# Seven products instead of eight in the down-projection of a hybrid decoder layer

## The chip, the cores and the metric

The kernel runs on one core of a Trainium2 chip. The metric is the device time of one execution in microseconds, as a median of several runs. A core has five engines that run side by side, each with a queue that it works through in order: TensorE (PE, matrix products, with its weight loads listed as PEld), VectorE (DVE), ScalarE (ACT), GpSimd (POOL) and SyncE (SP), which here starts nearly all DMA transfers. SBUF is the on-chip memory, 128 partitions wide; PSUM holds eight banks of 128 x 512 32-bit sums, into which TensorE alone accumulates matrix products.

## What is computed

One decoder layer with sequence length 2048, width 1024 and feed-forward width 2816, all in float32:

```python
def swiglu(h, w_gate_up, w_down):
    gu = h @ w_gate_up
    g, u = jnp.split(gu, 2, axis=-1)
    return (jax.nn.silu(g) * u) @ w_down
...
        h = modulate(rmsnorm(x, norm1_w[layer]), shift1, scale1)
        x = x + gate1[:, None, :] * hybrid_mixer(
            h, positions, w_in[layer], conv_w[layer], conv_b[layer], dt_bias[layer],
            a_log[layer], d_skip[layer], attn_sinks[layer], ssm_norm_w[layer], w_out[layer])
        h = modulate(rmsnorm(x, norm2_w[layer]), shift2, scale2)
        x = x + gate2[:, None, :] * swiglu(h, w_gate_up[layer], w_down[layer])
    return rmsnorm(x, final_norm_w)
```

The mixer (window attention beside a state-space scan, then an output projection by `w_out`) is left as it is by the change. What changes is the last product, `(silu(g) * u) @ w_down`, of 2048 x 2816 by 2816 x 1024, and the order of work around it.

## The kernel before

Everything is held transposed: features on the 128 partitions, tokens along the free axis. The 2048 tokens are four blocks of T = 512, and two blocks make a pair. Width 1024 is 8 slices of 128, the feed-forward width 22 slices (NF) of 128.

**Products.** A float32 operand is split into a high part (rounded to the matrix format, by ScalarE) and a low part (what is left, by VectorE or GpSimd). A product of a 128 x 128 weight with a 128 x 512 operand is three matmuls: high x high, high x low, low x high (`mm3`, lines 274 to 277). So each weight chunk of 128 x 512 from HBM costs a load of 256 KB into one of five `raw` buffers, one ScalarE and one VectorE or GpSimd operation into one of six `w` buffers, and then serves twelve matmuls.

**Gate and up.** `quads` runs 22 `quad`s for each pair of blocks. A quad makes slice f of the activations of both blocks, and does the 2 x 2 product of halves (two halves of the width 1024, two blocks) by seven products instead of eight, with sums of weights (`s1` to `s4`) and of tokens (`t1` to `t4`) in the manner of Strassen and Winograd. Its four sums stand in PSUM banks `pa` to `pd`. In the first pair these are always the same four `d` banks (the mixer's attention and scan of the last blocks run beside it and use the other four); in the second pair quads alternate between two sets of four. `u2`, `u3`, `c22`, `g1`, `g2`, `c12` are temporaries out of a ring of eight (`tmp`). The results are `g1` (first block, line 1010) and `g2` (second block, line 1005), and are written to DRAM (`act_d`, lines 1006 and 1011).

**Down.** `down(b)` runs for one block after the other: 6 groups of 4 (at last 2) activation slices, and in each group 8 columns of output. `acts` loads a group's activations and splits them (lines 1037 to 1040, ring `a` of 8); `columns` multiplies them with the split weights of that group and column, and at the end of every group adds the sum, times the gate, to the residual `x2` in SBUF (line 1075 on VectorE, reading PSUM). Block 0 writes its split weights to DRAM (`down_d`), block 1 reads them back, blocks 2 and 3 split anew. At the last group the squares of `x2` are summed for the final norm (`square_into`, ScalarE and GpSimd); `final` makes the root, spreads it over the partitions by a product with ones, scales, and writes the output. In block 3 the last group is done in two halves of 256 tokens, with VectorE in exactly the written order.

**Order.** `main` generators are stepped, and beside each step `beside` advances the generators in `sides` by a given ratio. A planner then orders each engine's instructions by when its own model of time has them ready, with the program's order as priority; inside `manual_schedule` the named engines keep the written order. From the first gate/up pair on, the order is: gate/up of blocks 0 and 1 with the attention and scan of the last blocks beside it, then the output projection of block 2 (`first_output`); `down` of blocks 0 and 1, with the rest of that projection, the projection of block 3 (`second_output`) and the second pair's operands (`first_operands`, `last_operands`) beside it; gate/up of blocks 2 and 3; `down` of blocks 2 and 3. `out_proj` (line 807) uses weights that block 0 split and kept in DRAM (512 KB per chunk, line 262).

## Time and profile before

| | us |
|---|---|
| median of three runs | 2342.59 (2342.11 to 2344.79) |
| span of the profiled execution | 2337.7 |
| gate/up of blocks 0 and 1, with mixer work beside it | 749.3 to 1322.6 |
| down of blocks 0 and 1, with output projections and operands beside it | 1322.6 to 1648 |
| gate/up of blocks 2 and 3 | 1648 to 2065.9 |
| down of blocks 2 and 3 | 2065.9 to 2323.8 |
| what is left after the last product | 2323.8 to 2337.7 |

The span runs from the first to the last instruction of one profiled execution. The page shows no other time for that execution than its span; the runs' times are taken apart from it, and the median is 4.9 above the span. The stages overlap a little at their edges, and the limits in the table are the starts of the first products of each. In rows of the profile, `d<-a,w` is a product of activations and down-projection weights, `d<-b,w` one of gate/up operands, and a name of the form L1075 is line 1075 of the kernel; `t<-act` is a load of an activation slice into a temporary.

### The profile page before, as it was taken

The numbers are of one execution on the slowest core, as the hardware profiler recorded it, in microseconds if no ns is written. First come the engines' busy times: TensorE is split into PE (matmuls) and PEld (weight loads), VectorE is DVE, ScalarE is ACT, GpSimd is POOL, SyncE is SP. The second block draws the span as 40 slices with busy tenths as digits, with TensorE's granted clock in tenths as the row PEclk, the third lists the DMA queues.
The fourth block names the chain that finished last, engine by engine and source line by source line (L and its number), as shares of the span: only waits on it lengthen the run. The fifth ranks groups of instructions, "written<-read, shape, count | busy, mean of one in ns | idle before, by whom it ended". The sixth has DMA issues, their size and how long they took to land. (4 is left out here: it accounts for less than half of the span.)

```text
span 2337.7 us, 33382 instructions
## 1 busy us (share of the span) xinstructions
PE 2233.3 (96%) x11252; PEld 1849.7 (79%) x11252; DVE 1444.3 (62%) x2607; ACT 943.0 (40%) x1976; POOL 1189.9 (51%) x1191
## 2 busy tenths in 40 slices
PE   6878989999999999999999999999999999999998
PEld 5778778888879788887877788877788888888777
DVE  8987975773568856676664353387644454454544
ACT  4564543654346645333333232223333333333332
POOL 2556433553223855687784332326666666653442
PEclk9998999999999999999999999999999999999999
DMA  8899987777888422323334998797422222263452
GB/s 295 291 327 306 304 260 250 252 247 252 293 268 314 135 86 73 108 86 95 95 100 154 337 359 307 238 340 244 140 82 81 82 82 81 81 226 104 134 182 64
DMA packets 271531, 453.14 MB, mean 194 GB/s; under 512 B 24960, under 2 KB 71040, under 8 KB 271360
## 3 DMA queue, kind: packets, MB, share of 16 engines
q1 hardware_dynamic: 270784, 450.48, 58.0%
q8 instruction: 89, 1.46, 0.3%
q14 instruction: 82, 0.67, 0.1%
q10 hardware_dynamic: 576, 0.52, 0.1%
HBM read 329.21 MB, written 121.70 MB: 193 GB/s over the span
## 5 line engine op out<-in xcount | busy, mean ns | idle before, releaser
L951 PE MATMUL d<-b,w 128*128 128x512 f32 x924 | 367.6, 399 | 1.3 <-POOL w L850 1.3
L950 PE MATMUL d<-b,w 128*128 128x512 f32 x924 | 366.8, 397 | 0.3 <-POOL b L880 0.3
L949 PE MATMUL d<-b,w 128*128 128x512 f32 x924 | 364.8, 398 | 1.1 <-DVE t L977 0.6
L849 ACT ACTIVATE w<-raw 128x512 fp32r<-128x512 f32 x264 | 166.0, 631 | 389.3 <-PE d L277 181.3
L275 PE MATMUL d<-a,w 128*128 128x512 f32 (+1 forms) x720 | 281.3, 393 | 6.1 <-ACT a L1039 3.2
L277 PE MATMUL d<-a,w 128*128 128x512 f32 (+1 forms) x720 | 282.8, 393 | 0.0
L276 PE MATMUL d<-a,w 128*128 128x512 f32 (+1 forms) x720 | 280.9, 390 | 1.1 <-POOL a L844 0.6
L1075 DVE SCALAR_TENSOR_TENSOR x<-d,mod,x 128x512 f32<-128x512 f32 (+1 forms) x182 | 130.8, 724 | 169.3 <-PE d L277 167.4
L850 DVE TENSOR_TENSOR w<-raw,w 128x512 fp32r<-128x512 f32 x198 | 184.8, 934 | 60.9 <-ACT w L849 57.0
L951 PEld LDWEIGHTS d<-b,w 128*128 128x128 f32 x924 | 174.1, 188 | 41.9 <-POOL w L850 1.7
L949 PEld LDWEIGHTS d<-b,w 128*128 128x128 f32 x924 | 174.4, 189 | 41.3 <-ACT t L980 1.2
L950 PEld LDWEIGHTS d<-b,w 128*128 128x128 f32 x924 | 174.5, 189 | 39.5 <-POOL b L880 0.7
L850 POOL TENSOR_TENSOR w<-s,w 128x512 fp32r<-128x512 f32 x132 | 187.3, 1420 | 31.5 <-ACT w L849 31.1
L849 ACT ACTIVATE w<-s 128x512 fp32r<-128x512 f32 x176 | 111.0, 632 | 221.1 <-PE d L951 163.1
L850 POOL TENSOR_TENSOR w<-raw,w 128x512 fp32r<-128x512 f32 x66 | 88.1, 1335 | 194.8 <-ACT w L849 173.5
L275 PE MATMUL d<-w,hl 128*128 128x256 f32 (+1 forms) x592 | 176.4, 298 | 7.3 <-ACT hl L326 5.6
L277 PE MATMUL d<-w,hl 128*128 128x256 f32 (+1 forms) x592 | 171.5, 290 | 2.7 <-DVE hl L327 2.7
L276 PE MATMUL d<-w,hl 128*128 128x256 f32 (+1 forms) x592 | 171.5, 290 | 0.0
L285 POOL TENSOR_TENSOR acc<-acc,t 128x512 f32<-128x512 f32 x70 | 95.8, 1369 | 147.7 <-ACT t L284 147.2
L275 PEld LDWEIGHTS d<-a,w 128*128 128x128 f32 x720 | 135.7, 189 | 40.0 <-ACT a L1039 5.4
L276 PEld LDWEIGHTS d<-a,w 128*128 128x128 f32 x720 | 136.3, 189 | 33.5 <-DVE a L844 1.1
L277 PEld LDWEIGHTS d<-a,w 128*128 128x128 f32 x720 | 135.8, 189 | 30.7 <-issue 0.7
(399 smaller groups left out, 5394.0 us busy)
## 6 DMA issues: line engine op xcount, KB each, us to landing
raw<-in_wgu_dram SPq DMA_DIRECT2D x176, 256.0 KB, 2.7
raw<-in_wd_dram SPq DMA_DIRECT2D x132, 256.0 KB, 2.9
w<-w_x SPq DMA_DIRECT2D x48, 512.0 KB, 5.1
w<-w_o SPq DMA_DIRECT2D x48, 512.0 KB, 5.2
act<-t SPq DMA_DIRECT2D x88, 256.0 KB, 2.1
wd<-w SPq DMA_DIRECT2D x88, 256.0 KB, 4.4
t<-act SPq DMA_DIRECT2D x88, 256.0 KB, 4.8
w<-wd SPq DMA_DIRECT2D x88, 256.0 KB, 4.2
```

The source lines that it names most:

```text
L275: nc.tensor.matmul(out, ahi, bhi, start=first, stop=False)
L276: nc.tensor.matmul(out, ahi, blo, start=False, stop=False)
L277: mm3.last = nc.tensor.matmul(out, alo, bhi, start=False, stop=last)
L285: eng.tensor_tensor(acc, acc, sq, ALU.add)
L849: nc.scalar.activation(hi, x, AF.Copy)
L850: eng.tensor_tensor(lo, x, hi.bitcast(F32), ALU.subtract)
L949: nc.tensor.matmul(out, ahi, bhi, start=first and k == 0, stop=False, skip_group_check=True)
L950: nc.tensor.matmul(out, ahi, blo, start=False, stop=False, skip_group_check=True)
L951: mm3.last = nc.tensor.matmul(out, alo, bhi, start=False, stop=k == 3, skip_group_check=True)
L1075: nc.vector.scalar_tensor_tensor(x, ps, gate2[:, c:c + 1], x, ALU.mult, ALU.add)
```

## The change

- The down-projection works on pairs of blocks too (class `pairs`). The 22 activation slices are two halves of 11 (KP; the even slices are one half, the odd the other), the 8 output columns two halves of 4. Seven products, each over the whole 11 slices, replace eight. Each is a stage: for each of 4 columns it goes through the weights in chunks of 4, 4 and 3 slices (`steps_of`), and a column's end is worked up in `done`.
- The token sums `t1` to `t4` are made in the quads, on VectorE, and written to DRAM beside `b11`, `b21`, `b22`; the even quad's two results are held until the odd quad's are there (`held`). The weight sums `s1` to `s4` are made beside the second pair's quads (`weight_sums`) and written to DRAM.
- A stage's 11 tokens are loaded and split while the stage before runs (`tokens_of`). Before the second pair's quads there is one ring of 11 buffers, after them two rings, of 11 and 12.
- Pair 0 does three products (b11, b21, t4) before the second gate/up pair and four after it; pair 1 does all seven after it. What the first three leave is kept in DRAM (`first_d`, `mid`).
- The last stage (`last`) goes through its columns twice, 256 tokens each time; its split weights are kept from the first time for the second. VectorE keeps the written order there. The early call of the square root's table is gone.
- The rest of the output projection of block 2 and that of block 3 run as main work in front of the down-projection, with loads of tokens and the first operands beside them. They split their weights anew from the input instead of reading the kept ones.
- Weights come as `wd` in one layout for all stages.

```diff
-    def weight(src, n, key, store, eng=nc.gpsimd):
+    def weight(src, n, key, store, eng=nc.gpsimd, fresh=False):
...
-        if key in split_d:
+        if key in split_d and not fresh:
...
-                whi, wlo = weight(wo[c, half], T, ("o", c, half), b == 0)
+                whi, wlo = weight(wo[c, half], T, ("o", c, half), b == 0, nc.gpsimd if half or b < 2 else nc.vector, b > 1)
...
-        nc.sync.dma_start(act_d[s][f, 1], g2)
+        if f % 2:
+            b11, b12 = held[s]
+            keep("b22", g2)
+            nc.vector.tensor_tensor(b12, g2, b12, ALU.subtract)
+            keep("t3", b12)
+            nc.vector.tensor_tensor(b11, b11, b12, ALU.add)
+            keep("t2", b11)
         yield
         turn(3)
         nc.vector.tensor_tensor(u3, u3, pa, ALU.add)
         nc.vector.tensor_tensor(g1, g1, u3, ALU.mult)
-        nc.sync.dma_start(act_d[s][f, 0], g1)
+        if f % 2:
+            keep("b21", g1)
+            nc.vector.tensor_tensor(u3, g1, b11, ALU.subtract)
+            keep("t4", u3)
+        else:
+            keep("b11", g1)
+            nc.vector.tensor_tensor(u3, g2, g1, ALU.subtract)
+            keep("t1", u3)
+            held[s] = g1, g2
...
+                nc.vector.tensor_tensor(a11, a11, a21, ALU.subtract)
+                nc.gpsimd.tensor_tensor(a21, a21, a22, ALU.add)
+                nc.vector.tensor_tensor(a22, a22, a11, ALU.subtract)
+                nc.gpsimd.tensor_tensor(a12, a12, a22, ALU.subtract)
...
+    def tokens_of(s, name, pool, n):
+
+        for k in range(KP):
+            hi, lo = pair("a", n, pool=pool)
+            raw = lo.bitcast(F32)
+            nc.sync.dma_start(raw, act_d[s][name][k])
+            nc.scalar.activation(hi, raw, AF.Copy)
+            flip[0] += 1
+            (nc.vector if flip[0] % 2 else nc.gpsimd).tensor_tensor(lo, raw, hi.bitcast(F32), ALU.subtract)
+            yield hi, lo
+
+    def steps_of(act, src, banks, new, done, ts=slice(0, T), kept_w=None):
+
+        turn = [0]
+        for c in range(4):
+            if new:
+                banks[c] = dense()
+            ps = banks[c][:, ts]
+            for lo, hi in CHUNKS:
...
+                    nc.scalar.activation(w[0], raw, AF.Copy)
+                    (nc.vector if turn[0] % 2 else nc.gpsimd).tensor_tensor(w[1], raw, w[0].bitcast(F32), ALU.subtract)
+                for k in range(lo, hi):
+                    ws = slice((k - lo) * P, (k - lo + 1) * P)
+                    for x, y in ((0, 0), (0, 1), (1, 0)):
+                        mm3.last = nc.tensor.matmul(ps, w[x][:, ws], act[k][y][:, ts], start=new and k == 0 and x + y == 0,
+                                                    stop=k == KP - 1 and x == 1, skip_group_check=True)
+                if hi == KP:
+                    done(c, ps)
+                yield
...
+            names = ("b11", "b21", "t4", "t2", "t3", "t1", "b22")
+            src = ((0, 0), (0, 1), (1, 1), "s2", "s3", "s1", "s4")[names.index(name)]
...
+                if name == "b11":
+                    u = self.u2[c] = big("u", 8, pool=self.pool) if self.pool else tmp()
+                    nc.scalar.activation(u, ps, AF.Copy)
+                    if not self.pool:
+                        nc.sync.dma_start(first_d[c], self.u2.pop(c))
+                elif name in ("b21", "t4"):
+                    i = int(name == "t4")
+                    self.residual(i, 0, c)
+                    added(i, 0, c, ps)
+                    if not self.pool:
+                        spilled(i, 0, c)
...
+                elif name == "t3":
+                    u = self.u3[c] = big("u", 8, pool=self.pool)
+                    nc.vector.tensor_tensor(u, self.u2[c], ps, ALU.add)
+                    added(1, 0, c, u)
+                    for i in range(2):
+                        squared(i, 0, c)
...
+                def done(c, ps):
+                    u, x = self.u2[c][:, ts], self.x[0, 1, c][:, ts]
+                    nc.vector.tensor_tensor(u, u, ps, ALU.add)
+                    nc.vector.scalar_tensor_tensor(x, u, gate(0, c), x, ALU.mult, ALU.add)
+                    n2, kept_sq = big("s", 3, pool=fw)[:, 0:T // 2], whole[:, ts]
                     nc.scalar.activation(n2, x, AF.Square)
-                    if c < KT - 2:
+                    if c < 2:
                         nc.gpsimd.tensor_tensor(kept_sq, kept_sq, n2, ALU.add)
                         return
...
+        for name, after in (("b11", "b21"), ("b21", "t4"), ("t4", None)):
+            nxt, coming = ring(0, after, dn, KP) if after else (None, None)
+            for i in beside(down0.stage(name, act), 0.5):
+                if after and i >= 8:
+                    for _ in range(4 if i < 10 else 3):
+                        next(coming, None)
...
+            if i >= 14 and i % 7 == 0:
+                next(sums_of, None)
+            if i >= 7 * NF - 12:
+                next(coming, None)
...
+    todo = [(down0, n) for n in ("t2", "t3", "t1", "b22")]
+    todo += [(down1, n) for n in ("b11", "b21", "t4", "t2", "t3", "t1", "b22")]
+    rings = ((dn, KP), (dn2, KP + 1))
```

More of the change, by code (lines that the diff above doesn't have):

```diff
@@ L834, in out_proj @@
         yield
-    act_d = [dr.tile([NF, 2, P, T], F32, name=f"act{s}") for s in range(2)]
+    act_d = [{n: dr.tile([KP, P, T], F32, name=f"act{s}_{n}") for n in ("b11", "b21", "b22", "t1", "t2", "t3", "t4")}
+             for s in range(2)]
+    held = {}
     flip = [0]
@@ L1092, in columns @@
                                              skip_group_check=True)
[L1094 to L1096 removed]
+                for i, _ in enumerate(steps_of(act, of, self.banks, False, done, ts, kept_w)):
+                    if part and i == 4:
+                        next(ends[0])
                     yield
[L1098 to L1107 removed]
@@ L1150, in norm_of_block_before, with final @@
-    def norm_of_block_before(b):
-        if b - 1 in finish_of:
+            for i in range(KT // 2):
+                next(ends[0])
+            next(ends[1])
+            drain(ends[0])
+            drain(ends[1])
+    def final(b, x2, ts, acc, last=False):
+        pool = final.pool
+        y = rstd(acc[:, ts], st=side_bank(2)) if b < NB - 1 else quick_root(acc, ts.stop // P - ts.start // P, pool)
+        if b < NB - 1:
+            yield
+        bc = spread(y, bc=side_bank(2 if last else 3))
+        if b == NB - 1:
+            yield
+        for d in range(KT):
+            x, o = x2[d][:, ts], tmp()[:, ts]
+            nc.vector.scalar_tensor_tensor(o, x, fw_[:, d:d + 1], bc, ALU.mult, ALU.mult)
+            (nc.scalar if last and d % 2 else nc.sync).dma_start(outT[b, d][:, ts], o)
+            if b == NB - 1:
+                yield
+        yield
@@ L1474, in hymba_layer @@
-        finish(last)
-        def next_acts():
-            acts_ahead[2, 0] = acts(2, 0, dn)
-        for i, _ in enumerate(quads(1, ops, lambda f: [side_bank(i) if f % 2 else dense() for i in range(4)], 0, next_acts)):
-            if i in (0, 2):
-                norm_of_block_before(2)
-    drain(down(2, dn, dn))
-    x3 = ctx.enter_context(tc.tile_pool(name="x3", bufs=1, reuse_waits="tile"))
-    drain(down(3, dn, x3))
+        act, coming = ring(0, "b11", dn, KP)
+        op3 = outputs.enter_context(tc.tile_pool(name="op3", bufs=1, side="right", reuse_waits="tile"))
@@ new lines, in hymba_layer @@
+        second = second_output()
+        next(second)
+        for i, _ in enumerate(first):
+            if i % 2:
+                next(coming, None)
+        sides[:] = [first_operands()]
+        for _ in beside(second, 0.3):
+            next(coming, None)
+        drain(coming)
+        finish(sides[0] if sides else None)
+        outputs.close()
+        bp = late.enter_context(tc.tile_pool(name="b1l", bufs=1, reuse_waits="tile"))
+        operand_tiles(ops, bp, ("t1", "b22", "t3", "t2", "t4"))
@@ new lines, in hymba_layer @@
+        act, coming = ring(0, "t2", dn, KP)
+        sums_of = weight_sums(ctx.enter_context(tc.tile_pool(name="wsum", bufs=1, side="right", reuse_waits="tile")))
+        for i, _ in enumerate(quads(1, ops, lambda f: [side_bank(i) if f % 2 else dense() for i in range(4)], 0)):
+            if i >= 14 and i % 7 == 0:
+                next(sums_of, None)
+            if i >= 7 * NF - 12:
+                next(coming, None)
+        drain(sums_of)
+        drain(coming)
+    dn2 = ctx.enter_context(tc.tile_pool(name="dn2", bufs=1, reuse_waits="tile"))
@@ new lines, in hymba_layer @@
+    down0.pool = down1.pool = final.pool = steps_of.spare = dn2
+    todo = [(down0, n) for n in ("t2", "t3", "t1", "b22")]
+    todo += [(down1, n) for n in ("b11", "b21", "t4", "t2", "t3", "t1", "b22")]
+    rings = ((dn, KP), (dn2, KP + 1))
+    for at, (d, name) in enumerate(todo):
+        nxt, coming = ring(todo[at + 1][0].s, todo[at + 1][1], *rings[(at + 1) % 2]) if at + 1 < len(todo) else (None, ())
+        coming = iter(coming)
+        is_last = at + 1 == len(todo)
+        with tc.manual_schedule(engines={mybir.EngineType.DVE}) if is_last else nullcontext():
+            for i, _ in enumerate(d.stage(name, act)):
+                if i in (2, 5):
+                    for b in list(finish_of):
+                        norm_of(b)
+                next(coming, None)
+        drain(coming)
+        act = nxt
```

270 lines of the change are left out of this document (125 added, 145 removed).

## The prediction

> **What bounds the kernel now.** I read the page's busy shares first, then the wait view filtered on TensorE over the stretch that the change rebuilds, then the busy times by stage.
>
> ```profile
> span 2337.7 us, 33382 instructions
> PE 2233.3 (96%) x11252; PEld 1849.7 (79%) x11252; DVE 1444.3 (62%) x2607; ACT 943.0 (40%) x1976; POOL 1189.9 (51%) x1191
> ...
> 749.30:1244.90 495.60, 484.10 (x2347) 394.60 (x2345) 318.70 (x468) 219.03 (x498) 347.33 (x338) 0.99 0.33 104
> 1322.60:1510.00 187.40, 187.36 (x817) 152.35 (x818) 81.82 (x129) 54.67 (x90) 65.81 (x49) 1.00 0.90 311
> 1510.00:1606.50 96.50, 89.30 (x369) 69.01 (x369) 81.39 (x123) 27.88 (x46) 33.86 (x23) 0.98 0.90 316
> 1648.00:2065.90 417.90, 417.63 (x1803) 337.81 (x1803) 218.26 (x261) 141.61 (x240) 262.01 (x189) 1.00 0.30 95
> 2065.90:2192.00 126.10, 126.10 (x545) 102.11 (x545) 63.10 (x86) 45.77 (x75) 54.79 (x40) 1.00 0.51 156
> 2192.00:2226.00 34.00, 31.63 (x131) 24.28 (x130) 21.53 (x40) 8.23 (x14) 12.22 (x10) 0.95 0.56 176
> 2226.00:2310.90 84.90, 84.90 (x367) 68.71 (x366) 38.48 (x53) 29.19 (x47) 31.47 (x23) 1.00 0.39 122
> 2310.90:2323.80 12.90, 12.90 (x111) 12.84 (x109) 8.65 (x23) 5.61 (x15) 5.43 (x8) 1.00 0.01 2
> ```
>
> The columns of a stretch are its length, then PE, PEld, DVE, ACT, POOL (busy us and instructions), granted clock, DMA share, GB/s. The stretches are: first gate/up pair; down-projections of blocks 0 and 1 (two rows, the second with the preparation of the second pair's operands); second gate/up pair; down-projections of blocks 2 and 3 (four rows, the last one in half-wide matmuls). TensorE is busy from end to end in nearly all of them, the others half the time. So the price of work is its TensorE time, and each wait of TensorE that is added counts in full. The pace: 84.90 us for 367 matmuls of 512 columns is 0.2313 us each, and 12.90 us for 111 is 0.116 us for the half-wide ones (half of the full one, so halving costs nothing).
>
> TensorE loses time in two places of the down-projections: 369 matmuls in 96.50 us should take 85.4 (11.1 lost), and 131 in 34.00 should take 30.3 (3.7 lost). In the first, VectorE is at 81.4 of 96.5.
>
> **The change: the matmuls.** Today: 4 blocks x 8 columns x 22 slices x 3 = 2112. After: 2 pairs x 7 products x 4 x 11 x 3 = 1848 full-wide equivalents (the last product's 132 as 264 halves, 30.6 us against 30.5). 264 fewer at 0.2313 is **-61.1 us**. Output projections keep their matmuls; they only move from beside the down-projection to in front of it. A stage (one product) is 132 x 0.2313 = 30.5 us, one slice-chunk of weights 12 x 0.2313 = 2.78 us.
>
> **The tail.**
>
> ```profile
> 2323.75 0.53 issue
> 2324.32 0.72 POOL kept_sq L1085
> 2325.09 0.77 POOLq L1534
> 2325.90 2.43 PE at L1090 x12
> 2319.96 0.42 ACT L1083 ACTIVATE s<-x 128x256 f32<-128x256 f32 x1 [0.83 <-POOL kept_sq L1085]
> ```
>
> After the last product (2323.78) the end waits for GpSimd's sums of squares, because columns end every 0.7 us and an addition takes 0.72 or more; then all 12 row-sum matmuls stand at the end. Afterwards the last columns are 33 x 0.116 = 3.8 us apart, so only the last square and a third of those matmuls remain (2.43 to 0.8), and one half-wide addition (0.48 at most) is new. I take -1.8, between 0 and -3. The table load for the square root that was made early (L1115) now comes in the middle of the last stage, under six or more weight chunks of matmuls with kept weights: nothing; if it were uncovered, its length in the trace, 1.28.
>
> ```profile
> L1115 ACT ACT_TABLE_LOAD x1 | 1.3, 1283 | 0.0
> L850 DVE TENSOR_TENSOR w<-raw,w 128x512 fp32r<-128x512 f32 x198 | 184.8, 934 | 60.9 <-ACT w L849 57.0 <-DMA wd<-w 3.2
> L1009 DVE TENSOR_TENSOR t<-t,d 128x512 f32<-128x512 f32 x33 | 22.5, 683 | 10.2 <-PE d L951 3.8 <-POOL t L999 3.0 <-POOL s L959 1.1
> L1010 DVE TENSOR_TENSOR t<-t 128x512 f32<-128x512 f32 x44 | 54.7, 1244 | 0.7
> L1075 DVE SCALAR_TENSOR_TENSOR x<-d,mod,x 128x512 f32<-128x512 f32 x166 | 123.4, 747 | 167.0 <-PE d L277 165.2 <-DMA x<-mid 1.3
> L844 POOL TENSOR_TENSOR a<-t,a 128x512 fp32r<-128x512 f32 x44 | 64.9, 1476 | 78.3 <-ACT a L1039 75.5 <-DMA wd<-w 2.1 <-DMA raw<-in_wd_dram 0.5
> L850 POOL TENSOR_TENSOR w<-raw,w 128x512 fp32r<-128x512 f32 x66 | 88.1, 1335 | 194.8 <-ACT w L849 173.5 <-DMA w<-w_o 4.8 <-DVE s L1075 4.3
> L1039 ACT ACTIVATE a<-t 128x512 fp32r<-128x512 f32 x88 | 53.4, 625 | 28.4 <-DMA t<-act 25.1 <-PE d L277 1.9
> L880 POOL TENSOR_TENSOR b<-t,b 128x512 fp32r<-128x512 f32 x28 | 42.6, 1530 | 17.4 <-ACT b L879 17.4
> t<-act SPq DMA_DIRECT2D x88, 256.0 KB, 4.8
> 1300.00:1350.00 50.00, 48.32 (x208) 38.55 (x207) 21.84 (x27) 15.14 (x25) 19.73 (x15) 1.00 1.02 365
> ```
>
> **A stage's side work.** 12 weight and 11 token splits: 23 x 0.63 = 14.5 us of ScalarE; 11.5 on VectorE at 0.93 = 10.7; 11.5 on GpSimd at 1.34 to 1.48 = 16; 23 loads of 256 KB in 30.5 us, 198 GB/s against the 365 of the last row. There are 168 weight and 154 token splits in place of 132 and 88, while evictions on VectorE fall from 192 to 64. All fits under 30.5, except where squares join: in t3 GpSimd has 8 more, 19.5 in all, 25.2 us at the uncontended 1.29 and 34.1 at 1.75, the durations of the rows below (VectorE's split alone 0.69). I take 1.5 us lost in each of two t3 stages: **+3** (0 to 7).
>
> ```profile
> 1163.50 0.68 DVE L850 TENSOR_TENSOR w<-raw,w 128x512 fp32r<-128x512 f32 x1
> 1172.27 1.29 POOL L850 TENSOR_TENSOR w<-s,w 128x512 fp32r<-128x512 f32 x1
> 1173.53 1.28 POOL L1005 TENSOR_TENSOR t<-t 128x512 f32<-128x512 f32 x1
> 1174.77 1.74 POOL L960 TENSOR_TENSOR s<-s,raw 128x512 f32<-128x512 f32 x1
> 1175.28 1.77 DVE L1010 TENSOR_TENSOR t<-t 128x512 f32<-128x512 f32 x1
> 1176.46 1.75 POOL L850 TENSOR_TENSOR w<-s,w 128x512 fp32r<-128x512 f32 x1
> ```
>
> The Trainium skill, SBUF — State Buffer, "Who interferes with whom", says that a VectorE instruction with two SBUF inputs and a GpSimd instruction that reads SBUF block one another fully. The trace agrees: L1010 (both inputs SBUF) takes 1.77 beside GpSimd, L1009 (one input PSUM) stays at 0.683. By that rule a t3 stage needs 19.5 x 1.29 + 11.5 x 0.69 = 33.1 us of one port, so 2.6 lost, +5 for two where I take +3; its full price is the second rival.
>
> **Waits added before the second gate/up pair.** The three stages b11, b21, t4 of pair 0 share one ring of 11 token buffers. A token's buffer is free after its last matmuls and wanted again 33 matmuls (7.6 us) later; 11 tokens and about 3 weight chunks are 3.7 MB, 10.1 us at 365 GB/s. SP's queue takes loads in order, so weight loads behind a token load that waits for its buffer wait too, and TensorE for them. That is 2.5 late at each of two changes of stage: **+5** (0, as six split weights stand ready, to 12).
>
> The second pair's operands (VectorE 36 operations of about 0.75, 27 us; GpSimd 16 at 1.53, 24.5 us) come at one step per two chunks, within 16 chunks or 44 us. With 8 weight splits and some 5 token splits each, and two evictions, that is VectorE 41 and GpSimd 43 of 44. Today's stretch at that density lost 11.1; I take 15: **+4** (-8 to +12). The output projections of blocks 2 and 3 split their weights anew, 0.63, and 0.93 or 1.34, per 2.78 us chunk, under TensorE's cover: 0; uncovered, one start of about 3 us. The 3.7 us lost between blocks 2 and 3 goes, as two token rings load a stage ahead: **-3.7** (-4 to +4). The 88 stores and 88 loads of split weights leave DMA; TensorE did not wait for them (187.36 of 187.40 at a DMA share of 0.90), so 0.
>
> **The last stage.** VectorE follows the written order there: the eviction of a column (0.683 + 0.747, then half-wide 0.48 + 0.48) stands ahead of the next weight's low part (0.69) where that falls to VectorE, at the stage's start and at the third column: 2.1 + 1.65, **+3.8** (0 to 6). TensorE stands behind it.
>
> **Beside gate/up.** Four additions per two quads (88, each 0.69 alone to 1.77) add 2.5 us to a quad's VectorE (318.7 of 495.6 and 218.3 of 417.9 used), and the weight sums 32 each on VectorE and GpSimd at two thirds of a normal width, about 1 us each, in the second pair. No engine fills. The first pair has one set of four banks, so a late eviction stops TensorE there; I take **+2** (0 to 15), the second pair 0. Two results held over use two of eight temporaries; the first output projections, some four quads, may wait for one: in the +2.
>
> **Sum.** -61.1 -1.8 +3 +5 +4 -3.7 +3.8 +2 = -48.8. The page shows a span of 2337.7 and no further time of its own run; the median is 4.9 above. 2337.7 - 48.8 = 2288.9, with the same 4.9 **2294 us**.
>
> **Rivals.** (1) The new waits hide: only the matmuls, the tail and the old gap count, -61.1 - 1.8 - 3.7, 2276. For it: six split and five raw weights stand ahead, 2.78 us each. Against: VectorE and GpSimd both full once. 0.17. (2) The shared port sets the pace: every GpSimd operation at 1.75. t3 loses 3.6 twice, the operands' 16 chunks need 29.5 x 1.75 = 51.6 for 44 and their backlog meets the ring change, some 15 beyond the sum: 2309. For it: DVE and POOL stretched in the rows above. Against: most stages have 8 us spare. 0.18. The rule of the Trainium skill named above would bring it about. (3) Slower: in each odd quad of the first pair the new differences (they need L1005's product) stand ahead of L1009 on VectorE, and L1009 frees the bank of the next quad's first product.
>
> ```profile
> 1169.94 1.22 DVE L1004 SCALAR_TENSOR_TENSOR t<-t 128x512 f32<-128x512 f32 x1 [0.70 <-ACT t L1003]
> 1172.95 0.68 DVE L1009 TENSOR_TENSOR t<-t,d 128x512 f32<-128x512 f32 x1
> ```
>
> L1005 ends at 1174.81; two differences at 1.244 move L1009 from 1172.95 to 1177.3, 4.35 us; with two more GpSimd operations ahead of L1005, 6.9. Over 11 odd quads 48 to 76: 2342 to 2370, about 2356. It decides from 4.4 us per odd quad (48.8 / 11). Against: the planner sees L1009 ready 1.9 us before L1005 ends, and orders by readiness. 0.05 (0.02 of it within 0.2%). That the work is not saved cannot be: the counts follow from the loops.
>
> **Chances.** The forecast has 0.60, within 2284 to 2304. The range reaches into (1) and (2): **2273 to 2314**. 0.2% (about 4.7 us) is what a measurement of this kernel can tell from no change. Faster 0.95, same 0.02, slower 0.03.
>
> **What would show it.** The matmuls that read token tiles fall from 2160 records to 1980 (264 of them half-wide); each late stage lasts 30.5 us with TensorE full. Gaps stand at the two ring changes (released by DMA or a split), in the operands' stretch, at the last stage's start (VectorE) and less in the tail. First gate/up at 484 busy of 496 or worse tells of (3). Wrong it would be if TensorE waited at every change of stage.

## The result, and the profile after

| | before | after |
|---|---|---|
| median of 4 runs (us) | 2342.35 (2339.60 to 2344.79) | 2351.98 (2349.26 to 2355.56) |
| span of the profiled execution | 2337.7 | 2347.6 |

The ratio is 1.0043 (95%: 1.0029 to 1.0057): a little slower. The forecast was 2294, its range ended at 2314, and the sign was wrong. One execution of nine of the experiment e3 below took 3679.57 us at a granted clock of 0.65; its median is 2337.95 with that one and 2337.66 without.

The page of the changed kernel, its span and busy shares:

```profile
span 2347.6 us, 33637 instructions
...
PE 2194.1 (93%) x11072; PEld 1817.4 (77%) x11072; DVE 1625.4 (69%) x2674; ACT 1006.1 (43%) x2113; POOL 1355.4 (58%) x1287
```

The groups of the down-projection's products, with different shapes apart (count, then busy us and mean ns of one, then idle before):

```profile
L1093 PE MATMUL d<-a,w 128*128 128x512 f32 x1716 | 412.6, 401 | 15.9 <-POOL a L1063 5.2 <-DVE w L1089 4.5 <-DVE a L1063 2.2
...
L1093 PE MATMUL d<-a 128*128 128x256 f32 x264 | 32.5, 284 | 0.0
```

The work is gone: 1716 full and 264 half products are 1848 full ones, 264 fewer than 2112. But TensorE's busy share fell from 96% to 93%, and VectorE's rose from 62% to 69%. The rows that answer to the busy times by stage shown of before (length, then PE, PEld, DVE, ACT, POOL, granted clock, DMA share, GB/s):

```profile
752.60:1258.90 506.30, 480.06 (x2324) 391.96 (x2322) 359.18 (x504) 218.46 (x497) 353.10 (x338) 0.98 0.35 112
1258.90:1527.30 268.40, 244.23 (x1007) 193.93 (x1008) 187.62 (x226) 113.19 (x195) 162.76 (x112) 0.95 0.67 226
1527.30:1973.90 446.60, 431.24 (x1826) 346.35 (x1825) 293.06 (x306) 145.69 (x249) 309.49 (x221) 0.98 0.43 138
1973.90:2302.60 328.70, 321.41 (x1376) 258.14 (x1375) 208.81 (x249) 146.75 (x265) 202.50 (x140) 0.99 0.68 229
```

They are: first gate/up pair; output projections and the three early stages; second gate/up pair; the ten late stages. At the 0.2313 us per matmul of before, the second row's 1007 should take 232.9 (35.5 lost), the third row's 1826 422.4 (24.2 lost), the fourth's 1376 318.3 (10.4 lost). In the first row TensorE was idle for 26.2, against 11.5 before.

Set against the terms of the forecast, each stretch from the start of its first products to the start of the next one's:

| stretch | before | after | change | foreseen |
|---|---|---|---|---|
| ahead of the first gate/up pair | 749.3 | 752.6 | +3.3 | 0 |
| first gate/up pair | 495.7 | 506.3 | +10.6 | +2 |
| output projections and down-projections, all stages | 653.6 | 630.0 | -23.6 | -49.0 |
| second gate/up pair | 425.3 | 446.6 | +21.3 | 0 |
| tail | 14.0 | 12.1 | -1.9 | -1.8 |

The last column is the forecast's -48.8, the changes make +9.7 of the 9.9 between the spans. The 3.3 ahead of the change's first effect is taken as no part of it: among the kernels run here that start lay between 746.7 and 754.9. The 425.3 of before counts from that pair's first product at 1639.7; the limit of 1648 in the table of the kernel before lies 8.3 after it.

The edges don't cut the same work everywhere. The first pair's last products run on beside the output projections, to 1333.6 (before: 1312.0), and 2324 matmuls stand ahead of the first output product against 2347 before. These 23 are 5.3 us at 0.2313, so for like work the first pair lost some 16 and not 10.6, and the row below it holds 5.3 more of work than the same row of before.

### Where the second gate/up pair loses its 24 us

The waits of TensorE from 1527 to 1700, then those of VectorE from 1545 to 1700 (waiting line, what it waited for: total us, times, longest):

```profile
PE am L954 <- DVE w L853: 7.0, 2, 3.5
PE d L952 <- ACT t L975: 5.8, 2, 4.7
```

```profile
DVE ws L1047 <- DMA ws<-in_wd_dram: 22.6, 9, 4.2
DVE ws L1049 <- POOL ws L1048: 9.5, 5, 3.5
```

TensorE waits for an eviction on ScalarE (L975) and for splits on VectorE (L853). VectorE in its turn stands at the weight sums: L1046 loads them, L1047 and L1049 are on VectorE, L1048 and L1050 on GpSimd, L1052 stores. The view of that tile (durations min/median/max in ns, first and last start):

```profile
L1046 SPq DMA_DIRECT2D ws<-in_wd_dram x64: 327/412/1316, 1422.2 to 1662.5; - x64
...
L1052 SPq DMA_DIRECT2D wd_s<-ws x64: 319/327/795, 1426.8 to 1670.4; - x64
```

The program's text spreads the sixteen steps over the second pair, one per quad from the third quad on. The planner moved them up, to 1422 to 1670. The pool `ws` has four buffers and a step uses all four, so the next step's loads wait for this step's stores. The chain of waits that ends in TensorE's longest wait shows it (start, us, what):

```profile
1606.79 2.52 DMA ws<-in_wd_dram
...
1609.47 0.96 POOL ws L1050
...
1612.11 3.12 DMA wd_s<-ws
...
1615.24 2.35 DMA ws<-in_wd_dram
...
1620.98 2.69 DMA ws<-in_wd_dram
...
1623.79 0.65 DVE ws L1047
1624.45 0.61 DVE t L1008
...
1625.08 0.64 ACT t L1009
```

Load, sum, store, load again. VectorE had nothing to do for 4.22 us before L1047, but the quad's own L1008 was queued behind it; ScalarE's L1009 waited for L1008, and the eviction L975 was queued behind L1009. TensorE's timeline there (idle before in brackets):

```profile
1626.24 0.79 PE L952 MATMUL d<-b,w 128*128 128x512 f32 x1 [4.73 <-ACT t L975]
1626.84 0.63 PE L953 MATMUL d<-b,w 128*128 128x512 f32 x1
1627.26 0.63 PE L954 MATMUL d<-b,w 128*128 128x512 f32 x1
...
1629.40 0.52 PE L953 MATMUL d<-b,w 128*128 128x512 f32 x1
```

The wait costs twice: for 3.2 us after it the matmuls start 0.43 apart instead of 0.23 (granted clock 0.50 in that stretch). Of the 24.2 lost, 15.4 are idle (446.60 - 431.24) and 8.8 are such slow matmuls (431.24 - 422.4).

### Where the output projections and the early stages lose 35

The longest wait is at the output projection of block 3; waits of TensorE, then VectorE's timeline:

```profile
PE at L276 <- DVE t L821: 10.2, 1, 10.2
PE d L1093 <- POOL a L1063: 5.2, 1, 5.2
...
PE d L1093 <- DVE w L1089: 3.8, 1, 3.8
```

```profile
1352.38 0.69 DVE L255 TENSOR_TENSOR mo<-t,mo 128x512 fp32r<-128x512 f32 x1 [2.21 <-ACT mo L254]
...
1357.97 0.74 DVE L821 SCALAR_TENSOR_TENSOR t<-at,mod,t 128x512 f32<-128x512 f32 x1
```

The eviction L821 is queued behind the splits (L255) of block 3's mixer results, whose loads have taken the temporaries that the residual's load needs too. L1063 and L1089 are the token and weight splits of the early stages, where the ring of 11 turns over. Of the 35.5 lost, 24.2 are idle (268.40 - 244.23) and 11.3 slow matmuls.

Two more waits stand just ahead of this stretch, at the end of the first pair, from 1246.7 to 1258.9: one for the scan's last root (L794) and one for the splits of block 2's mixer results (L254). With the scan's other waits they are most of the 26.2 that TensorE was idle in the first pair. The waits of that stretch after the change, then before it:

```profile
PE st L715 <- ACT m L794: 6.8, 1, 6.8
PE sm L780 <- DVE m L709: 4.6, 3, 2.1
PE am L276 <- ACT mo L254: 4.3, 1, 4.3
PE st L768 <- DVE m L761: 3.5, 2, 2.0
```

```profile
PE sm L779 <- DVE m L708: 2.7, 1, 2.7
...
PE am L275 <- ACT mo L253: 1.2, 1, 1.2
...
PE st L714 <- ACT m L793: 0.3, 1, 0.3
```

L779, L708, L275, L253, L714 and L793 of before are L780, L709, L276, L254, L715 and L794 after; a wait like that of L768 is not there before. In sum these are 19.2 after the change and 4.2 before.

### The profile page after: what moved, and what is told of

Its sections match the earlier page's. It is cut to its first block, busy times and chain, and to the rows that moved or that the text cites. A ratio compares the mean times of both kernels' runs of the same rounds, so it can differ in the third digit from the quotient of the medians.

```text
span 2347.6 us, 33637 instructions
## 1 busy us (share of the span) xinstructions
PE 2194.1 (93%) x11072; PEld 1817.4 (77%) x11072; DVE 1625.4 (69%) x2674; ACT 1006.1 (43%) x2113; POOL 1355.4 (58%) x1287
## 5 line engine op out<-in xcount | busy, mean ns | idle before, releaser
L1093 PE MATMUL d<-a,w 128*128 128x512 f32 x1716 | 412.6, 401 | 15.9 <-POOL a L1063 5.2
L1093 PEld LDWEIGHTS d<-a,w 128*128 128x128 f32 x1716 | 326.9, 191 | 98.6 <-POOL a L1063 5.6
L853 POOL TENSOR_TENSOR w<-s,w 128x512 fp32r<-128x512 f32 x132 | 190.6, 1446 | 15.7 <-ACT w L852 11.6
L276 PE MATMUL d<-w,hl 128*128 128x256 f32 (+1 forms) x592 | 176.6, 298 | 8.6 <-ACT hl L327 6.4
L1089 POOL TENSOR_TENSOR w<-raw,w 128x512 fp32r<-128x512 f32 (+1 forms) x78 | 112.8, 1449 | 86.8 <-ACT w L1088 86.7
L968 POOL TENSOR_TENSOR s<-raw,s 128x512 f32<-128x512 f32 x44 | 58.8, 1337 | 174.3 <-DVE w L853 86.7
L269 POOL TENSOR_TENSOR w<-raw,w 128x512 fp32r<-128x512 f32 (+1 forms) x68 | 94.7, 1394 | 97.8 <-ACT w L268 89.2
L853 DVE TENSOR_TENSOR w<-raw,w 128x512 fp32r<-128x512 f32 x132 | 138.3, 1050 | 17.7 <-ACT w L852 16.6
L276 PE MATMUL d<-hl,w 128*128 128x512 f32 x352 | 147.2, 418 | 3.2 <-ACT w L268 2.2
L1063 DVE TENSOR_TENSOR a<-a 128x512 fp32r<-128x512 f32 x77 | 104.5, 1372 | 62.7 <-ACT a L1061 56.7
L278 PE MATMUL d<-hl,w 128*128 128x512 f32 x352 | 141.2, 401 | 1.4 <-DVE w L269 0.7
L277 PE MATMUL d<-hl,w 128*128 128x512 f32 x352 | 140.7, 400 | 0.0
```

What stands on the lines that cost most here:

```text
L276: nc.tensor.matmul(out, ahi, bhi, start=first, stop=False)
L277: nc.tensor.matmul(out, ahi, blo, start=False, stop=False)
L278: mm3.last = nc.tensor.matmul(out, alo, bhi, start=False, stop=last)
L853: eng.tensor_tensor(lo, x, hi.bitcast(F32), ALU.subtract)
L1063: (nc.vector if flip[0] % 2 else nc.gpsimd).tensor_tensor(lo, raw, hi.bitcast(F32), ALU.subtract)
L1089: (nc.vector if turn[0] % 2 else nc.gpsimd).tensor_tensor(w[1], raw, w[0].bitcast(F32), ALU.subtract)
```

## The experiments

My theory was that the gain was lost to side work placed in front of what TensorE waits for: (A) weight sums, (B) token sums, as in the forecast's third rival, (C) the fresh weights and the loads of the output projections, (D) the turns of the one token ring. The rival theory was that the work itself fills the engines, wherever it stands. Stretches in us, each from first product to first product; late stages are the ten:

| kernel | median | ratio to before (95%) | first gate/up | outputs | early stages | second gate/up | late stages |
|---|---|---|---|---|---|---|---|
| after | 2351.98 | 1.0043 (1.0029 to 1.0057) | 506.3 | 153.9 | 114.5 | 446.6 | 328.7 |
| e1_no_sums | 2318.27 | 0.9903 (0.9882 to 0.9924) | 508.1 | 152.3 | 114.1 | 423.0 | 324.5 |
| e2_no_diffs | 2322.56 | 0.9914 (0.9896 to 0.9932) | 501.0 | 145.0 | 118.1 | 439.2 | 325.9 |
| e3_kept_wo | 2337.95 | 0.9980 (0.9965 to 0.9995) | 499.8 | 149.8 | 120.4 | 442.5 | 323.4 |
| e4_same_tokens | 2337.35 | 0.9977 (0.9959 to 0.9996) | 505.3 | 152.0 | 100.7 | 451.8 | 325.9 |
| f1_dn_ring | 2341.76 | 1.0000 (0.9986 to 1.0014) | 505.4 | 154.5 | 112.5 | 442.2 | 323.6 |
| f3_dn_assign_kept | 2332.27 | 0.9957 (0.9938 to 0.9975) | 501.0 | 151.0 | 118.9 | 437.4 | 328.9 |
| f4_dn_assign_kept_spread | 2334.59 | 0.9968 (0.9957 to 0.9979) | 504.1 | 142.6 | 125.2 | 437.7 | 326.9 |
| g1_psum_diffs | 2314.53 | 0.9892 (0.9877 to 0.9908) | 481.8 | 150.5 | 115.5 | 442.3 | 323.7 |
| h1_sums_spaced | 2328.08 | 0.9942 (0.9925 to 0.9960) | 503.6 | 154.1 | 115.5 | 429.3 | 324.3 |
| h2_late_diffs | 2347.35 | 1.0022 (1.0008 to 1.0035) | 509.6 | 152.2 | 114.6 | 449.7 | 324.4 |
| h3_spaced_late_kept | 2323.64 | 0.9923 (0.9905 to 0.9942) | 498.3 | 152.0 | 119.0 | 429.5 | 324.9 |
| h4_no_sums_no_diffs | 2304.78 | 0.9845 (0.9828 to 0.9863) | 499.4 | 145.8 | 115.2 | 422.6 | 324.7 |
| i1_inplace | 2339.78 | 0.9995 (0.9982 to 1.0009) | 505.2 | 147.9 | 114.9 | 449.4 | 325.8 |
| i2_h3_inplace | 2320.28 | 0.9903 (0.9886 to 0.9921) | 500.1 | 142.7 | 124.9 | 429.5 | 325.6 |
| i3_h3_inplace_slow | 2319.65 | 0.9904 (0.9891 to 0.9917) | 502.3 | 142.2 | 123.0 | 429.7 | 327.2 |

Differences of kernels below are between medians; the stretches come from one execution each. Executions of one kernel lay up to 18 us apart (e4: 2329.92 to 2348.06), and the one with the stretches was 7.4 below the median in e4 and 5.1 above it in i1. So a few us are not to be read out of a single number here.

Two edges move. In the kernels with kept output-projection weights (e3, f3, f4, h3, i2, i3) the first token product comes 5.8 to 13.7 us ahead of the projections' last product, so there only the sum of outputs and early stages can be compared. And e2 and h4 have 24 matmuls (5.6 us) more in the first pair and fewer in the outputs than the others.

### Weight sums left out

```diff
-                return sum_d[src][c] if isinstance(src, str) else wd[c + 4 * src[0], src[1]]
+                return wd[c, 1] if isinstance(src, str) else wd[c + 4 * src[0], src[1]]
...
-            if i >= 14 and i % 7 == 0:
-                next(sums_of, None)
...
-        drain(sums_of)
```

> The weight sums are left out (no loads, no additions, no stores; the stages that used a sum read plain weights instead, so three of seven products are of other weights). Theory A, the sums' own chain: VectorE and GpSimd work in order and stand at the sums' loads (VectorE 22.6 us at line 1047 between 1527 and 1690), so the second gate/up pair falls from 451 us to about 420 and the whole by 30 to 40, to 2312 to 2322. Theory B, the port shared by VectorE and GpSimd is full because of all that was added: the sums are 64 small operations of some 2300, so 5 to 10 less, 2342 to 2347.

Measured: 33.7 us less. The second gate/up pair by itself:

```profile
1523.60:1946.60 423.00, 423.00 (x1826) 343.20 (x1825) 262.54 (x283) 146.92 (x250) 281.06 (x198) 1.00 0.32 105
```

The same 1826 matmuls, TensorE busy in all of the 423.0, clock 1.00. 23.6 of the 33.7 come from this stretch: the sums were the whole loss there.

### Token sums left out

```diff
-            nc.vector.tensor_tensor(b12, g2, b12, ALU.subtract)
...
-            nc.vector.tensor_tensor(b11, b11, b12, ALU.add)
...
-            nc.vector.tensor_tensor(u3, g1, b11, ALU.subtract)
...
-            nc.vector.tensor_tensor(u3, g2, g1, ALU.subtract)
```

> The four additions per two quads that make the token sums are left out; the same tiles are stored and held, so the token sums are wrong. Theory A: 5 to 10 less, nearly all in the first gate/up pair, the second pair still at about 445. Theory B (and the rival that VectorE's held differences delay the first pair's evictions): the first pair loses 15 or more, the second another 10 or more, in all 25 to 35 less, 2317 to 2327.

Measured: 29.4 less, but spread: 14.2 in the first pair and the outputs together (some 11 of it in the first pair for like work), 7.4 in the second pair. In the first pair the wait for L794 fell from 6.8 to 0.8, and that for L761 is gone. Without any addition the first pair is still 5.3 longer than before the change, with as many matmuls.

### Kept weights for the output projections

```diff
-                whi, wlo = weight(wo[c, half], T, ("o", c, half), b == 0, nc.gpsimd if half or b < 2 else nc.vector, b > 1)
+                whi, wlo = weight(wo[c, half], T, ("o", c, half), b == 0)
```

> The output projections of blocks 2 and 3 read the kept split weights again instead of splitting anew. If the fresh splits (raw buffers, VectorE and GpSimd time) cause the waits at 1253 (11 us in two) and 1348 to 1359 (10.2 us behind VectorE), 10 to 20 less. If those waits come from the loads of block 3's mixer results ahead of the residual's load and from the end of the scan, within 4 us of the changed kernel.

Measured: 14.0 less, but none of it in the outputs and early stages, which together are 1.8 longer: the wait at L821 rose from 10.2 to 12.1. The first pair is 6.5 shorter, 5.1 of it in the wait for L794 (6.8 to 1.7), the second pair 4.1, the late stages 5.3. So splitting anew was not free, but its price stood mostly outside the projections; why the second pair and the late stages gain is open.

### The same tokens for all three early stages

```diff
-            nxt, coming = ring(0, after, dn, KP) if after else (None, None)
+            after = None
...
-                act = nxt
+                pass
```

> Stages b21 and t4 of pair 0 use the tokens of b11 again, so 22 token loads and splits and both turns of the single ring are gone (two products have other tokens). If the turns of the ring cost what 1446 to 1475 shows (about 11 us of waits for token and weight splits), 10 to 14 less. If those waits come from the second pair's operands and the hoisted weight sums beside them, 5 or less.

Measured: 14.6 less, and the early stages 13.8 shorter. Two turns of the ring, with their loads and splits, cost 13.8 and not 5. The second pair became 5.2 longer, so not all of it was won.

### The additions with one operand from PSUM

```diff
-            nc.vector.tensor_tensor(b12, g2, b12, ALU.subtract)
+            nc.vector.tensor_tensor(b12, g2, pd, ALU.subtract)
...
-            nc.vector.tensor_tensor(b11, b11, b12, ALU.add)
+            nc.vector.tensor_tensor(b11, b11, pd, ALU.add)
...
-            nc.vector.tensor_tensor(u3, g1, b11, ALU.subtract)
+            nc.vector.tensor_tensor(u3, g1, pd, ALU.subtract)
...
-            nc.vector.tensor_tensor(u3, g2, g1, ALU.subtract)
+            nc.vector.tensor_tensor(u3, g2, pd, ALU.subtract)
```

> The four additions per two quads stay, on VectorE, with the same stores and after the same results, but the second operand of each is read from the PSUM bank pd in place of SBUF, so the token sums hold other numbers. If the 29 us that the additions cost come from the port that VectorE and GpSimd share (an SBUF pair 1.2 to 1.8 us and GpSimd stretched, a PSUM operand 0.68), most of it goes: 2325 to 2335. If they come from VectorE's order (evictions behind additions that wait for GpSimd's product), the order and its waits stay: 2345 to 2352.

Groups of VectorE, two of the four additions in after, then one of them in this kernel; behind them this kernel's first gate/up pair:

```profile
L1029 DVE TENSOR_TENSOR t<-t 128x512 f32<-128x512 f32 x22 | 33.6, 1525 | 2.5 <-POOL t L1011 1.2
...
L1025 DVE TENSOR_TENSOR t<-t 128x512 f32<-128x512 f32 x22 | 19.1, 869 | 0.2
```

```profile
L1029 DVE TENSOR_TENSOR t<-t,d 128x512 f32<-128x512 f32 x22 | 15.0, 683 | 6.4 <-POOL t L1011 4.8 <-DVE t L1022 0.5
```

```profile
753.70:1235.50 481.80, 476.59 (x2323) 389.67 (x2322) 345.23 (x512) 220.47 (x504) 346.50 (x336) 1.00 0.37 118
```

An addition falls from 0.87 to 1.53 us to 0.68, and the kernel gains 37.5. The Trainium skill, SBUF — State Buffer, "Who interferes with whom", says that a VectorE instruction with at most one SBUF input, outside its two-port modes, does not contend with GpSimd; the durations agree. But the first pair is 24.5 shorter than after's, with as many matmuls, and for like work some 14 shorter than with no additions at all. Less blocking can't beat having nothing to block. The waits at the end of the scan, 6.8 and 4.3 in after, are gone here, and without additions the 4.3 stayed. The planner orders all engines anew for each text, so the order of work can be behind the rest; that is argued and not shown, and what share of the 37.5 is the port is open.

### Sums through the deeper token ring

```diff
-                a11, a21, a22, a12 = (small([P, n], "ws", 4, pool=pool) for _ in range(4))
+                a11, a21, a22, a12 = (x.bitcast(F32)[:, 0:n] for _ in range(2) for x in pair("a", KP, pool=pool))
...
-        sums_of = weight_sums(ctx.enter_context(tc.tile_pool(name="wsum", bufs=1, side="right", reuse_waits="tile")))
+        sums_of = weight_sums(dn)
```

> All work is kept; the weight sums use the token ring (11 pairs, two to a step, free in the second gate/up pair) in place of their own four tiles, so five steps can be loaded ahead. Theory A (each step's load waits for the stores of the step before, and VectorE and GpSimd stand at it): most of what leaving the sums out gave comes back, 2318 to 2328. If the sums cost by their operations and the port: 2340 to 2350.

Measured: 10.2 less, 4.4 of it in the second pair. VectorE's wait for the loads of the sums fell from 25.3 to 9.4, but the sums stood closer together still, from 1521 to 1620: more buffers alone don't undo the planner's place.

### With the second sum on VectorE and kept weights, and then with the loads spread

The first of the two is the kernel above, with e3's line and

```diff
-                nc.gpsimd.tensor_tensor(a21, a21, a22, ALU.add)
+                nc.vector.tensor_tensor(a21, a21, a22, ALU.add)
```

> As the kernel with the sums in the token ring, and with the second sum moved from GpSimd to VectorE (no step in which VectorE waits for GpSimd to have read an operand), and the output projections on kept split weights. If the losses add: 10 to 16 below the kernel with the ring alone, 2305 to 2315, under both kernels.

The second also spreads block 3's loads over the projection of block 2.

```diff
         for c in range(KT):
             loaded(3, c, op3)
-        yield
+            if c % 2:
+                yield
...
-        next(second)
...
+            elif i < 8:
+                next(second)
```

> As the one before, and the loads and splits of block 3's mixer results spread over the steps of block 2's projection instead of all ahead of it. If VectorE's wait of 10 us at 1348 to 1358 comes from these splits standing ahead of the eviction: another 6 to 10 less. If the kept weights had taken that wait away already: the same within 4.

Measured: 2332.27 and 2334.59. The first is 9.5 below the kernel with the ring alone, and 17 above the 2315 at which the expected range ended. Spreading won nothing: the projections take 156.3 from their first to their last product, against 156.7, and outputs and early stages together are 2.1 shorter. The wait at L821 shrank from 12.8 to 7.0, and one of 8.5 for a token split came up behind it.

### Weight sums one step per quad, behind the quad's results

Loads one step ahead, through the token ring; the additions are tied behind the quad's two results, three on VectorE and one on GpSimd.

```diff
+        def added(c, cs, a11, a21, a22, a12):
+            with tc.issue_after(mark["dve"].ins), tc.issue_after(mark["pool"].ins):
...
+                got = [x.bitcast(F32)[:, 0:n] for _ in range(2) for x in pair("a", KP, pool=pool)]
+                with tc.issue_after(mark["sp"].ins):
+                    for x, (i, h) in zip(got, ((0, 0), (1, 0), (1, 1), (0, 1))):
+                        nc.sync.dma_start(x, wd[c + 4 * i, h][:, cs])
+                if ahead:
+                    added(*ahead)
+                ahead = c, cs, *got
```

> All work is kept. The weight sums use the token ring, each step's loads go out one quad before its additions, and both are tied behind the results of a quad, one step a quad; three of the four additions on VectorE, so that it never waits for GpSimd there. With the ring alone the 16 steps were bunched into 1516 to 1605. If waits at loads and the bunching are what the sums cost, the second gate/up pair falls to about 425 us (423 without any sums) and the whole to 2318 to 2328. If it is their operations wherever they stand, it stays at 2335 to 2345.

The second gate/up pair, and then the group of the first of the sums on VectorE:

```profile
1524.70:1954.00 429.30, 424.81 (x1825) 343.92 (x1824) 293.51 (x331) 146.15 (x250) 300.92 (x213) 1.00 0.49 159
```

```profile
L1044 DVE TENSOR_TENSOR a<-a 128x352 f32<-128x352 f32 x16 | 25.8, 1613 | 0.0
```

VectorE does as much in this stretch as after's (293.51 against 293.06), this sum takes 1.61 us each time, and yet the stretch is 17.3 shorter: VectorE stands idle for 0.0 ahead of the sum, where after's stood 22.6. So of the 23.6 that the sums cost in this stretch, 17.3 hung on where, from which buffers and on which engine they are done; the ring alone gave 4.4 (f1). The 6.3 that stay are one wait of 4.5 for a split (L853) and the slow matmuls behind it. In the whole kernel 23.9 of the 33.7 came back. The rival theory, that the work fills the engines wherever it stands, has the smaller part.

### Token sums behind the first result

```diff
-            nc.vector.tensor_tensor(b12, g2, b12, ALU.subtract)
-            keep("t3", b12)
-            nc.vector.tensor_tensor(b11, b11, b12, ALU.add)
-            keep("t2", b11)
...
+            with tc.issue_after(done.ins):
+                nc.vector.tensor_tensor(b12, g2, b12, ALU.subtract)
+                nc.vector.tensor_tensor(b11, b11, b12, ALU.add)
```

> The same additions for the token sums, but the two that stand between the third and fourth turn of an odd quad are tied behind the fourth turn's evictions, so no eviction stands behind them on VectorE. Order theory (my rival of VectorE held ahead of the first pair's evictions): 10 to 25 less than the changed kernel, most of it in the first pair, 2327 to 2342. Port theory (each addition takes 0.9 to 1.5 us and blocks wherever it stands): within 5 of the changed kernel, 2347 to 2355.

Measured: 4.6 less, and the first pair is 3.3 longer. The forecast's third rival put 48 to 76 on two additions standing ahead of the eviction; taking them away from there gives nothing in that stretch. Nor does TensorE wait anywhere in after's first pair for L1021, which is the rival's L1009. So that was not the mechanism, and it is luck that the sign came out as the rival had it.

### Together

h3 is h1, h2 and e3 in one. h4 leaves out both kinds of sums, as e1 and e2 do.

> Spaced sums, late differences and kept output-projection weights together, all work kept. If the parts add: 2352 less 25 to 30 (sums), 0 to 20 (order) and 5 to 14 (kept weights), 2290 to 2320, under the kernel before. If one bottleneck only passes on to the next: no better than the best single part.

> Neither weight sums nor token sums are made (the products read plain weights and whatever the held tiles have). If these two side jobs are what separates the prediction from the result, and add (34 and 29): 2284 to 2296, at the predicted 2294. If the loss has another source that both only hid: 2305 or more.

Measured: h3 28.3 less, where h1 alone gave 23.9; the parts don't add. h4 47.2 less, where e1 and e2 by themselves add up to 63: the effects overlap. So the two kinds of sums make 47 of the 58 between forecast and result. At 2304.8 h4 lies 11 above the forecast; that the sum of the other terms comes so near says nothing of each of them.

### Block 3's loads past the temporaries

```diff
-            loaded(3, c, op3)
+            hi, lo = pair("mo", KT, pool=op3)
+            raw = lo.bitcast(F32)
+            nc.sync.dma_start(raw, spill[3][c])
+            nc.scalar.activation(hi, raw, AF.Copy)
+            nc.vector.tensor_tensor(lo, raw, hi.bitcast(F32), ALU.subtract)
+            mixes[3].append((hi, lo))
```

> The changed kernel with one edit: block 3's mixer results are loaded straight into their operand buffers and split there, as tokens are, in place of going through the eight temporaries. If the 10.2 us wait at line 821 comes from those temporaries (the residual's load gets none until they are split), it goes and the kernel falls by 6 to 12, to 2340 to 2346. If it comes from VectorE's splits standing ahead of the eviction, they still stand there: within 4 of 2352.

```profile
PE at L276 <- DVE t L821: 4.7, 1, 4.7
```

Measured: 12.2 less by the medians (4.4 between the two spans), the wait at L821 fell from 10.2 to 4.7 and the outputs by 6.0. So loading past the temporaries takes away about half of that wait; the splits still stand ahead of the eviction, and 4.7 are left.

i2 puts this into h3, and i3 slows the second pair's operands beside the early stages from 0.5 to 0.3 steps per chunk.

> The same edit on the kernel with spaced sums, late differences and kept weights (2323.6, with a wait of 12.8 at line 821). If the parts add: 2311 to 2318. If it only passes on to the next wait: 2320 to 2326.

> As the one before, with the second pair's last operands at 0.3 of a step per chunk in place of 0.5. If VectorE and GpSimd, both full in that stretch, cause the waits at the turns of the single ring (some 12 us), 4 to 8 less. If the turns themselves do, or the operands then come too late for the second gate/up pair: the same within 3, or more.

Measured: 2320.28 and 2319.65, the same within their spread, so the rate of the operands is not what holds the early stages. i2 is 3.4 below h3, so most of what i1 gave by itself passed on to other waits. It beats both kernels: 0.9903 (0.9886 to 0.9921) of the time before. What it still waits for, in the same view:

```profile
PE at L276 <- DVE t L821: 9.2, 2, 5.3
PE d L1103 <- ACT a L1071: 7.5, 1, 7.5
```

## Why the prediction was wrong, by its own steps

**"The second pair 0" is the step that failed most.** It weighed the weight sums as busy time ("No engine fills"), and their busy time was near its estimate: the groups of L1047 to L1050 hold 14.7, 18.2, 21.8 and 19.5 us, 1.16 each against "about 1 us". What it left out is that an engine works in order: it never asked how deep the ring of the loads was (one step), whether the planner would keep "one per quad" (it did not), or what was queued behind a sum that waits for its load. Shown: 23.6 in that stretch by leaving the sums out, 17.3 of it won back by placing and buffering them otherwise and moving one of the four additions to VectorE; 33.7 and 23.9 for the whole kernel.

**"I take +2" for the token sums.** Their busy time was right: 106.0 us over 44 quads is 2.4 a quad against 2.5. Leaving them out gave 29.4. The step asked for late evictions of the quads only, and that is not what came (h2). What TensorE waited for in the first pair is the scan beside it and the splits behind its end: 19.2 us against 4.2 before in the four waits shown above. The forecast had no term for side work that delays other side work. Both the additions and the fresh splits have a part in it: without the one the wait for L794 is 0.8, without the other 1.7, in place of 6.8. How much of it is the shared port and how much the planner's order stays open (g1); the stretch lay between 481.8 and 509.6 in kernels with the same products.

**The ring changes, +5, and the operands' stretch.** The mechanism of the turns was there, the size off: 13.8 (e4). That the three early stages came out as foreseen is luck: 410 matmuls in 114.5 us are 19.7 lost, against 5 for the turns and 15 for the operands, but without the turns only 5.8 are lost (410 matmuls in 100.67). The turn also needs 11 token splits, which stood beside the second pair's operands and the first weight sums. VectorE's timeline in that stretch shows them at the 1.75 to 1.77 that the forecast's rows gave beside a busy GpSimd:

```profile
1451.19 1.75 DVE L1063 TENSOR_TENSOR a<-a 128x512 fp32r<-128x512 f32 x1
1452.87 1.75 DVE L938 TENSOR_TENSOR t<-t 128x512 f32<-128x512 f32 x1
```

**The output projections, 0.** Their stretch lost 15.4 (599 matmuls in 153.9 us), 10.2 of it in the wait at L821. Kept weights gave 14.0 in the whole kernel (e3) but nothing in this stretch; loading block 3 past the temporaries gave 12.2, 6.0 of it here (i1). The forecast looked at TensorE's cover per chunk, not at the temporaries that loads and evictions share.

The single effects, 33.7 + 29.4 + 14.0 + 14.6 + 12.2 = 104, are more than the 58 between forecast and result. They overlap: where one wait goes, another is late next, as f4 and e4 showed.

**What was right.** The matmuls: 264 fewer, and where TensorE is full the pace is that of before (the last 288 us of the second pair):

```profile
1690.00:1978.00 288.00, 288.00 (x1243) 233.39 (x1242) 174.97 (x191) 96.30 (x163) 183.87 (x131) 1.00 0.31 102
```

288.00 / 1243 is 0.2317. The tail fell by 1.9, against 1.8. Of the t3 stages one was hit and one not, 6.3 and 0 against 1.5 each:

```profile
2010.00:2045.00 35.00, 30.86 (x124) 23.75 (x124) 21.67 (x20) 16.56 (x31) 25.52 (x18) 0.95 0.72 246
2240.00:2271.00 31.00, 31.00 (x135) 25.11 (x135) 18.20 (x19) 15.71 (x29) 24.15 (x18) 1.00 0.57 187
```

In the first, 124 x 0.2313 is 28.7 of 35.0; the second is full. GpSimd, which the forecast had at 25 to 34 us of work there, was busy for 25.5 of 35.0 and 24.2 of 31.0, so it was full in neither. For the last stage the number is near and the reason wrong: it took 2.4 longer than its 264 x 0.116 = 30.6 against 3.8 foreseen, but TensorE waited for VectorE nowhere in it; 1.1 of the 2.4 are the three groups of row sums that moved in from the tail.

## What to carry to other kernels

When side work is put beside a stage whose bound is another engine, don't price it by busy shares: for each instruction that waits, ask what is queued behind it on its engine, how many steps its ring of buffers holds, and whether the scheduler will keep the place that the program's text gives it. Ask it for the other side work too: in the first pair here it was the scan that came late. A step whose loads, sums and stores share one set of buffers pays a full memory round trip with the engine standing in line; one step ahead in a deeper ring, tied behind the results that others need, gave back some 70% of the price here. And leave out one part at a time and compare stretch by stretch, since single effects overlap.

## What the runs showed of the hardware

Waits of TensorE are dearer than their length. After the waits of 3.45, 3.52 and 4.73 us in the second gate/up pair, matmuls started 0.43 apart in place of 0.23 for three to six microseconds (granted clock 0.50 after the 3.45 and the 4.73); after those of 0.77 and 1.38 they did not:

```profile
1586.14 0.79 PE L954 MATMUL am<-b,w 128*128 128x512 f32 x1 [3.45 <-DVE w L853]
...
1591.85 0.52 PE L954 MATMUL d<-b,w 128*128 128x512 f32 x1
...
1656.75 0.50 PE L954 MATMUL d<-b,w 128*128 128x512 f32 x1 [1.38 <-DVE w L853]
```

The Trainium skill, TensorE: Matmul & The Clock Gate, "Part 1: The HAM clock gate (the "warmup" mystery)", says that the clock falls to half after an idle window of about 3.4 us and comes back after about 3.4 us of steady work. This trace by itself fits the first: 3.45 us was enough to lose it, 1.38 was not; 3.2 to 5.7 us passed until it was back, so up to more than the page's figure. But shorter waits lost it too. In f3, matmuls started 0.43 apart for 3.4 us behind a wait of 2.02 and, but for the first step, 0.23 apart right behind one of 2.43:

```profile
1570.15 0.62 PE L952 MATMUL d<-b,w 128*128 128x512 f32 x1 [2.02 <-ACT t L975]
1570.57 0.63 PE L953 MATMUL d<-b,w 128*128 128x512 f32 x1
```

```profile
1601.99 0.50 PE L954 MATMUL d<-b,w 128*128 128x512 f32 x1 [2.43 <-DVE w L853]
1602.32 0.39 PE L952 MATMUL d<-b,w 128*128 128x512 f32 x1
```

So the measurement decides against 3.4 us as the least wait that counts; from what length on a wait costs the clock, these runs don't show. The forecast counted each wait at its own length.

The second thing is how far one stretch moves when only VectorE's work beside it changes: the first gate/up pair took 481.8 us in g1 and 509.6 in h2, with 2323 and 2324 matmuls in it, and g1 makes 44 additions in it that e2, at 501.0, leaves out.
